# Cross-entropy over 32000 columns: the labels' logits by a masked sum on VectorE, with a third buffer, a fixed order and short loads at both ends

## Chip, cores, metric

One core of a Trainium2 chip. The metric is the time on the device in microseconds (us), the median of several runs. A profiled execution gives a page and a trace; its span is about 1.8 us shorter than the time of the same execution.

## The reference

```python
batch, seq, vocab = 16, 512, 32000            # logits float32, labels integer
logits_max = np.max(logits, axis=-1, keepdims=True)
log_sum_exp = np.log(np.sum(np.exp(logits - logits_max), axis=-1)) + logits_max.squeeze(-1)
loss = -(logits - log_sum_exp[..., None])[np.arange(batch)[:, None], np.arange(seq), labels]
```

There are 8192 rows of 32000 logits: 1.05 GB to read once. For each row the kernel needs the log of the sum of exp, and one single logit, that of the label. Logits are drawn from a normal distribution, so both kernels leave out the maximum.

## The kernel before

A partition holds 64 rows; "group" g is row g of every partition (128 rows). A group is loaded in two pieces of 128x16000, the last three groups in pieces of 128x4000. ScalarE takes exp in place and sums it on the way. The labels' logits come by 64 indirect DMAs (gathers) of 128 single numbers.

```python
data_pool = ctx.enter_context(tc.tile_pool(name="data", bufs=2))     # 128x16000
fine_pool = ctx.enter_context(tc.tile_pool(name="fine", bufs=5))     # 128x4000
nc.sync.dma_start(out=labs64[:], in_=labels_pg)
# ... idx = row * V + label
for g in range(G):
    nc.gpsimd.indirect_dma_start(out=lab_logit[:, g:g + 1], out_offset=None, in_=lg,
        in_offset=bass.IndirectOffsetOnAxis(ap=idx[:, g:g + 1], axis=1))
for g in range(G):
    # the last three groups: the same in 8 pieces of WF = 4000 from fine_pool
    for c in range(C):
        t = data_pool.tile([P, W], FP32)                             # W = 16000
        nc.sync.dma_start(out=t[:], in_=lg_pg[:, g, c * W:(c + 1) * W])
        nc.scalar.activation(out=t[:], in_=t[:], func=Exp, accum_out=stats_col(g, c))
# ... finalize(): sum of stats, Ln on ScalarE, minus lab_logit, store
finalize(0, G - 1)
finalize(G - 1, G)
```

The softmax here doesn't subtract the row's maximum and nothing guards it: scores larger than these inputs give would overflow.

## Time and profile before

| | before |
|---|---|
| median time | 2440.22 us (2440.01 to 2440.32) |
| span of the profiled execution | 2438.7 us |
| bytes from memory | 1048.7 MB, 430 GB/s over the span |
| share of the 16 DMA engines taken by the load queue | 99.6% |

The profile's page of the kernel before: busy time by engine (us, share, instructions), and the DMA queues (packets, MB, share of 16 engines' time). Queue q1 carries the loads, q0 the gathers, q14 the instructions that the engines fetch.

```profile
span 2438.7 us, 851 instructions
...
DVE 1.7 (0%) x5; ACT 1754.4 (72%) x298; POOL 61.2 (3%) x70
...
## 3 DMA queue, kind: packets, MB, share of 16 engines
q1 hardware_dynamic: 21168, 1048.65, 99.6%
q0 software_dynamic: 2048, 0.04, 0.1%
...
q14 instruction: 6, 0.05, 0.0%
```

ScalarE is busy for 72% and VectorE hardly at all (1.7 us): the transfers set the time. This is the table of stretches for before: the stretch, its length, busy time of VectorE, ScalarE and GpSimd (instructions), granted clock, DMA share, GB/s.

```profile
core 0: us, DVE busy (x) ACT busy (x) POOL busy (x), PEclk, DMA share, GB/s
0.00:100.00 100.00, 0.48 (x1) 55.80 (x9) 27.25 (x34) 1.00 1.00 419
100.00:200.00 100.00, 0.00 (x0) 70.85 (x11) 22.62 (x24) 1.00 0.99 421
200.00:300.00 100.00, 0.00 (x0) 72.68 (x11) 11.31 (x12) 1.00 1.01 430
300.00:1300.00 1000.00, 0.00 (x0) 719.74 (x107) 0.00 (x0) 1.00 1.00 433
```

The first 300 us, in which GpSimd issues the gathers, move 419 to 430 GB/s; after that it is 433 throughout. The DMA share is 0.99 to 1.01 in all: the engines hardly wait, but the packets take longer. The packet records of the trace say it more sharply. A row of a 16000-wide load is one packet of 64000 bytes; its mean is 2.424, 2.399 and 2.389 us in the three stretches of 100 us with gathers, and 2.365 us from then on.

The end of the timeline of before: start, duration, engine, line, operation, and in brackets what the engine had waited for. The last exp and the store that ends the kernel:

```profile
2430.84 3.54 ACT L76 ACTIVATE tf<-tf 128x4000 f32<-128x4000 f32 x1 [1.11 <-DMA tf<-in_logits_dram]
...
2436.21 0.34 ACTq L109 DMA_DIRECT2D out_dram<-res  x1
```

The last load lands at 2430.84 us; the span ends 7.9 us later.

### The profile page before, as it was taken

Reading aid. Unit: us, or ns where it says so; the run is one execution under the profiler, and the core shown is the slowest. Engines: PE = TensorE matmul, PEld = TensorE weight load, DVE = VectorE, ACT = ScalarE, POOL = GpSimd, SP = SyncE. Lnnn points to the kernel's source line nnn. Section 1 sums busy time; section 2 is a strip of 40 time slices with the busy share of each in tenths; the row PEclk is TensorE's granted clock in tenths of the full one; section 3 lists DMA queues with packets and bytes.
Section 4 is the critical chain, followed back from the end, with each engine's and each line's share of the span. In section 5 each row is a group of like instructions: output and inputs, shape, how many; then the busy total and the mean of one; then the engine's idle time right before and its main releaser. Section 6 shows DMA issues by size and latency. Waiting matters only on the chain.

```text
span 2438.7 us, 851 instructions
## 1 busy us (share of the span) xinstructions
DVE 1.7 (0%) x5; ACT 1754.4 (72%) x298; POOL 61.2 (3%) x70
## 2 busy tenths in 40 slices
DVE  0000000000000000000000000000000000000000
ACT  4777766777677767777677767777677767777697
POOL 3222000000000000000000000000000000000000
DMA  9999999999999999999999999999999999999998
GB/s 404 437 420 422 435 437 435 429 429 437 437 436 428 431 435 437 435 432 428 435 436 436 435 427 434 436 437 435 427 432 436 437 435 425 434 437 432 426 430 360
DMA packets 23510, 1048.77 MB, mean 430 GB/s; under 512 B 4688, under 2 KB 4816, under 8 KB 4816
## 3 DMA queue, kind: packets, MB, share of 16 engines
q1 hardware_dynamic: 21168, 1048.65, 99.6%
q0 software_dynamic: 2048, 0.04, 0.1%
q10 hardware_dynamic: 288, 0.03, 0.0%
q14 instruction: 6, 0.05, 0.0%
HBM read 1048.67 MB, written 0.03 MB: 430 GB/s over the span
## 4 chain that ended last, share of the span: by engine, by line
DMA 63%; ACT 36%; issue 0%; ACTq 0%; SPq 0%; DVE 0%
DMA t<-in_logits_dram 61%; ACT t L85 34%; DMA tf<-in_logits_dram 2%; ACT tf L76 2%; ACT L101 0%; ACT L76 0%; ACTq L85 0%; ACT logsum L101 0%; SPq L84 0%; DVE res L105 0%; SPq L48 0%; ACTq L109 0%; ACTq L76 0%
## 5 line engine op out<-in xcount | busy, mean ns | idle before, releaser
L85 ACT ACTIVATE t<-t 128x16000 f32<-128x16000 f32 x122 | 1651.4, 13536 | 642.9 <-DMA t<-in_logits_dram 642.9
L76 ACT ACTIVATE tf<-tf 128x4000 f32<-128x4000 f32 x24 | 84.7, 3530 | 14.6 <-DMA tf<-in_logits_dram 14.6
L57 POOL DMA_INDIRECT lab_logit<-in_logits_dram,idx x64 | 60.5, 945 | 186.8 <-DMA lab_logit<-in_logits_dram,idx 184.2
L85 ACT ACTIVATION_READ_ACCUMULATOR t<-t 128x1 f32 x122 | 22.7, 186 | 0.0
L85 ACT ACT_TABLE_LOAD x1 | 1.3, 1283 | 23.3 <-DMA t<-in_logits_dram 23.3
L76 ACT ACTIVATION_READ_ACCUMULATOR tf<-tf 128x1 f32 x24 | 4.5, 187 | 0.0
L101 ACT ACT_TABLE_LOAD x2 | 2.6, 1283 | 0.0
L96 DVE TENSOR_REDUCE totals<-stats 128x63 f32<-128x504 f32 x1 | 0.7, 678 | 2394.9 <-ACT tf L76 2394.9
L76 ACT ACT_TABLE_LOAD x1 | 1.3, 1283 | 0.8 <-DVE res L105 0.8
L66 DVE MEMSET stats<- 128x504 f32 x1 | 0.5, 478 | 0.9 <-PEq L127 0.9
L101 ACT ACTIVATE logsum<-totals 128x63 f32<-128x63 f32 (+1 forms) x2 | 0.5, 229 | 0.0
L105 DVE TENSOR_TENSOR res<-logsum,lab_logit 128x63 f32<-128x63 f32 (+1 forms) x2 | 0.4, 192 | 2.2 <-ACT logsum L101 2.2
L53 POOL TENSOR_TENSOR idx<-idx,labs 128x64 int32<-128x64 int32 x1 | 0.3, 318 | 1.8 <-DMA labs<-in_labels_dram 1.8
L96 DVE TENSOR_REDUCE totals<-stats_last 128x1 f32<-128x8 f32 x1 | 0.2, 161 | 36.4 <-ACT tf L76 36.4
L51 POOL IOTA idx<- 128x64 int32 x1 | 0.2, 172 | 0.4 <-PEq L138 0.4
L127 POOL MEMSET const-uint8-127<- 128x1 uint8 x1 | 0.1, 118 | 0.0
L127 POOL MEMSET const-bfloat16-1.0<- 128x1 bf16 x1 | 0.1, 113 | 0.0
L127 POOL MEMSET const-float32-0.0<- 128x1 f32 x1 | 0.1, 98 | 0.2 <-issue 0.2
L127 POOL MEMSET const-float32-1.0<- 128x1 f32 x1 | 0.1, 104 | 0.0
## 6 DMA issues: line engine op xcount, KB each, us to landing
t<-in_logits_dram SPq DMA_DIRECT2D x122, 8000.0 KB, 24.1
tf<-in_logits_dram SPq DMA_DIRECT2D x24, 2000.0 KB, 20.1
lab_logit<-in_logits_dram,idx POOLq DMA_INDIRECT x64, 33.4
labs<-in_labels_dram SPq DMA_DIRECT2D x1, 64.0 KB, 1.9
out_dram<-res ACTq DMA_DIRECT2D x1, 31.5 KB, 9.1
out_dram<-res ACTq DMA_DIRECT2D x1, 0.5 KB, 1.4
```

What stands on the lines that cost most here:

```text
L51: nc.gpsimd.iota(idx[:], pattern=[[V, G]], base=0, channel_multiplier=G * V)
L53: nc.gpsimd.tensor_tensor(out=idx[:], in0=idx[:], in1=labs32, op=mybir.AluOpType.add)
L57: nc.gpsimd.indirect_dma_start(out=lab_logit[:, g:g + 1], out_offset=None, in_=lg, in_offset=bass.IndirectOffsetOnAxis(ap=idx[:, g:g + 1], ...
L66: nc.vector.memset(stats[:], 0.0)
L76: nc.scalar.activation(out=tf[:], in_=tf[:], func=mybir.ActivationFunctionType.Exp, accum_out=stats_col(g, c),)
L85: nc.scalar.activation(out=t[:], in_=t[:], func=mybir.ActivationFunctionType.Exp, accum_out=stats_col(g, c),)
L96: nc.vector.reduce_sum(out=totals[:, lo:hi], in_=stats[:, lo:hi, :] if hi <= G - 1 else stats_last[:], axis=mybir.AxisListType.X,)
L101: nc.scalar.activation(out=logsum[:, lo:hi], in_=totals[:, lo:hi], func=mybir.ActivationFunctionType.Ln,)
L105: nc.vector.tensor_tensor(out=res[:, lo:hi], in0=logsum[:, lo:hi], in1=lab_logit[:, lo:hi], op=mybir.AluOpType.subtract,)
L127: nc = _bacc.Bacc("TRN2", target_bir_lowering=False, num_devices=1)
```

## The change

The intent: take the label logits out of the data that pass through the chip anyway, on the idle VectorE. For 4000 columns at a time, VectorE compares the column number with the label and multiplies the outcome with the logits; the sum is the label's logit or zero. That saves 62 of the 64 gathers. Around it: a third wide buffer, three short loads first, ten shrinking loads last, exp in halves of 8000 (each waits for two masked sums, as exp overwrites the logits), one table set for exp and log (ScalarE loads a table four times in before, 1.28 us each, and once in after), and program order on all engines. Core of the diff:

```diff
-    data_pool = ctx.enter_context(tc.tile_pool(name="data", bufs=2))
-    fine_pool = ctx.enter_context(tc.tile_pool(name="fine", bufs=5))
+    GG = G - 2
+    plan(0, [[4000, 4000, 8000], [16000]], [(0, 0), (0, 1), (0, 2), (1, 0)])
+    for g in range(1, G - 2):
+        plan(g, [[W], [W]], [(0, 0), (1, 0)])
+    plan(G - 2, [[W], [10000, 6000]], [(0, 0), (1, 0), (1, 1)])
+    plan(G - 1, [[7400, 5840, 2260], [4540, 3720, 2920, 1780, 1460, 1120], [960]], ...)
+    data = ctx.enter_context(tc.tile_pool(name="data", bufs=3))
+    masked = psum.tile([P, H], FP32)                      # H = 4000
+    cols = persist.tile([P, H], mybir.dt.uint16)          # 0 .. 3999
-    nc.sync.dma_start(out=labs64[:], in_=labels_pg)
+    nc.scalar.dma_start(out=labs64[:], in_=labels_pg)
+    nc.scalar.preload_act_table_set("natural_log_exp_and_others")
-    for g in range(G):
+    for g in range(GG, G):
         nc.gpsimd.indirect_dma_start(...)
...
+        nc.sync.dma_start(out=t[:, at:at + n], in_=lg_pg[:, g, c0:c0 + n])
+        if g < GG:
+            for i in range(n // H):
+                h = c0 // H + i
+                lo = at + i * H
+                nc.vector.scalar_tensor_tensor(
+                    out=masked[:], in0=cols[:], scalar=lab_at[:, h, g:g + 1],
+                    in1=t[:, lo:lo + H], op0=ALU.is_equal, op1=ALU.mult,
+                    accum_out=found[:, g, h:h + 1])
+                if n == W and i % 2 == 1:
+                    exp(g, t[:, lo - H:lo + H])
+            if n < W:
+                exp(g, t[:, at:at + n])
+        else:
+            exp(g, t[:, at:at + n])
...
+    nc.scalar.activation(out=logsum_last[:], in_=sums_last[:, K - 1:K], func=LN, bias=part[:])
```

More of the change, by code (lines that the diff above doesn't have):

```diff
@@ L7 @@
 from concourse._compat import with_exitstack
+from concourse.masks import make_identity
 FP32 = mybir.dt.float32
 I32 = mybir.dt.int32
+EXP = mybir.ActivationFunctionType.Exp
+LN = mybir.ActivationFunctionType.Ln
+ALU = mybir.AluOpType
+X = mybir.AxisListType.X
 @with_exitstack
@@ L23 @@
     B, S, V = logits.shape
-    N = B * S
     P = 128
-    G = N // P
-    assert N % P == 0
+    G = B * S // P
     W = 16000
-    C = V // W
-    assert V % W == 0
-    WF = 4000
-    CF = V // WF
-    FINE_GROUPS = 3
-    assert V % WF == 0
+    H = 4000
+    NH = V // H
     lg = logits.rearrange("b s v -> (b s) v")
@@ L41, with plan @@
     out_pg = out.rearrange("b s -> (b s)").rearrange("(p g) -> p g", g=G)
-    data_pool = ctx.enter_context(tc.tile_pool(name="data", bufs=2))
-    fine_pool = ctx.enter_context(tc.tile_pool(name="fine", bufs=5))
+    GG = G - 2
+    loads = []
+    def plan(g, widths_by_buffer, order):
+        n_buffers = 1 + max((l[1] for l in loads), default=-1)
+        for b, i in order:
+            ws = widths_by_buffer[b]
+            loads.append((g, n_buffers + b, sum(ws[:i]), ws[i]))
+    plan(0, [[4000, 4000, 8000], [16000]], [(0, 0), (0, 1), (0, 2), (1, 0)])
@@ L45 @@
+    for g in range(1, G - 2):
+        plan(g, [[W], [W]], [(0, 0), (1, 0)])
+    plan(G - 2, [[W], [10000, 6000]], [(0, 0), (1, 0), (1, 1)])
+    plan(
+        G - 1,
+        [[7400, 5840, 2260], [4540, 3720, 2920, 1780, 1460, 1120], [960]],
+        [(0, 0), (0, 1), (1, 0), (1, 1), (1, 2), (0, 2), (1, 3), (1, 4), (1, 5), (2, 0)],
+    )
+    assert sum(l[3] for l in loads) == G * V
+    data = ctx.enter_context(tc.tile_pool(name="data", bufs=3))
     persist = ctx.enter_context(tc.tile_pool(name="persist", bufs=1))
+    psum = ctx.enter_context(tc.tile_pool(name="psum", bufs=1, space=bass.MemoryType.PSUM))
@@ L47 @@
+    masked = psum.tile([P, H], FP32)
     labs64 = persist.tile([P, G], mybir.dt.int64)
-    nc.sync.dma_start(out=labs64[:], in_=labels_pg)
-    idx = persist.tile([P, G], I32)
-    nc.gpsimd.iota(idx[:], pattern=[[V, G]], base=0, channel_multiplier=G * V)
     labs32 = labs64[:].bitcast(I32).rearrange("p (g two) -> p g two", two=2)[:, :, 0]
-    nc.gpsimd.tensor_tensor(out=idx[:], in0=idx[:], in1=labs32, op=mybir.AluOpType.add)
+    cols = persist.tile([P, H], mybir.dt.uint16)
+    idx = persist.tile([P, G - GG], I32)
@@ L55 @@
+    lab_at = persist.tile([P, NH, G], FP32)
+    found = persist.tile([P, GG, NH], FP32)
     lab_logit = persist.tile([P, G], FP32)
-    for g in range(G):
+    K = 10
+    sums = persist.tile([P, G - 1, 5], FP32)
+    sums_last = persist.tile([P, K], FP32)
+    totals = persist.tile([P, G - 1], FP32)
+    logsum = persist.tile([P, G - 1], FP32)
+    res = persist.tile([P, G - 1], FP32)
+    part = persist.tile([P, 1], FP32)
+    logsum_last = persist.tile([P, 1], FP32)
+    res_last = persist.tile([P, 1], FP32)
@@ L57 @@
+    ctx.enter_context(tc.manual_schedule())
+    nc.scalar.dma_start(out=labs64[:], in_=labels_pg)
+    nc.scalar.preload_act_table_set("natural_log_exp_and_others")
+    nc.vector.memset(sums[:], 0.0)
+    nc.gpsimd.iota(cols[:], pattern=[[1, H]], base=0, channel_multiplier=0)
+    nc.gpsimd.iota(idx[:], pattern=[[V, G - GG]], base=GG * V, channel_multiplier=G * V)
+    nc.gpsimd.tensor_tensor(out=idx[:], in0=idx[:], in1=labs32[:, GG:G], op=ALU.add)
+    for g in range(GG, G):
         nc.gpsimd.indirect_dma_start(
@@ L60 @@
             in_=lg,
-            in_offset=bass.IndirectOffsetOnAxis(ap=idx[:, g:g + 1], axis=1),
+            in_offset=bass.IndirectOffsetOnAxis(ap=idx[:, g - GG:g - GG + 1], axis=1),
         )
-    stats = persist.tile([P, G - 1, CF], FP32)
-    stats_last = persist.tile([P, 1, CF], FP32)
-    nc.vector.memset(stats[:], 0.0)
-    def stats_col(g, c):
-        return stats[:, g, c:c + 1] if g < G - 1 else stats_last[:, 0, c:c + 1]
-    for g in range(G):
-        if g >= G - FINE_GROUPS:
-            for c in range(CF):
-                tf = fine_pool.tile([P, WF], FP32)
-                nc.sync.dma_start(out=tf[:], in_=lg_pg[:, g, c * WF:(c + 1) * WF])
-                nc.scalar.activation(
-                    out=tf[:], in_=tf[:],
-                    func=mybir.ActivationFunctionType.Exp,
-                    accum_out=stats_col(g, c),
-                )
-        else:
-            for c in range(C):
-                t = data_pool.tile([P, W], FP32)
-                nc.sync.dma_start(out=t[:], in_=lg_pg[:, g, c * W:(c + 1) * W])
-                nc.scalar.activation(
-                    out=t[:], in_=t[:],
-                    func=mybir.ActivationFunctionType.Exp,
-                    accum_out=stats_col(g, c),
-                )
@@ L91 @@
-    totals = persist.tile([P, G], FP32)
-    logsum = persist.tile([P, G], FP32)
-    res = persist.tile([P, G], FP32)
-    def finalize(lo, hi):
-        nc.vector.reduce_sum(
-            out=totals[:, lo:hi],
-            in_=stats[:, lo:hi, :] if hi <= G - 1 else stats_last[:],
-            axis=mybir.AxisListType.X,
-        )
-        nc.scalar.activation(
-            out=logsum[:, lo:hi], in_=totals[:, lo:hi],
-            func=mybir.ActivationFunctionType.Ln,
-        )
-        nc.vector.tensor_tensor(
-            out=res[:, lo:hi], in0=logsum[:, lo:hi], in1=lab_logit[:, lo:hi],
-            op=mybir.AluOpType.subtract,
-        )
-        nc.scalar.dma_start(out=out_pg[:, lo:hi], in_=res[:, lo:hi])
@@ L111, with exp @@
-    finalize(0, G - 1)
-    finalize(G - 1, G)
+    for h in range(NH):
+        nc.vector.tensor_scalar(
+            out=lab_at[:, h, :], in0=labs32, scalar1=float(-h * H), scalar2=None, op0=ALU.add
+        )
+    buffers = {}
+    col = {}
+    n_exp = {}
+    def exp(g, ap):
+        k = n_exp.get(g, 0)
+        n_exp[g] = k + 1
+        s = sums[:, g, k:k + 1] if g < G - 1 else sums_last[:, k:k + 1]
+        nc.scalar.activation(out=ap, in_=ap, func=EXP, accum_out=s)
+    for j, (g, b, at, n) in enumerate(loads):
+        if b not in buffers:
+            buffers[b] = data.tile([P, W], FP32, tag="t", name="t")
+        t = buffers[b]
+        c0 = col.get(g, 0)
+        col[g] = c0 + n
+        nc.sync.dma_start(out=t[:, at:at + n], in_=lg_pg[:, g, c0:c0 + n])
[4 more added lines that the diff above has]
+                nc.vector.scalar_tensor_tensor(
+                    out=masked[:],
+                    in0=cols[:],
+                    scalar=lab_at[:, h, g:g + 1],
+                    in1=t[:, lo:lo + H],
+                    op0=ALU.is_equal,
+                    op1=ALU.mult,
+                    accum_out=found[:, g, h:h + 1],
+                )
+                if n == W and i % 2 == 1:
+                    exp(g, t[:, lo - H:lo + H])
+            if n < W:
+                exp(g, t[:, at:at + n])
+        else:
+            exp(g, t[:, at:at + n])
+        left = len(loads) - 1 - j
+        if left == 6:
+            nc.vector.reduce_sum(out=totals[:], in_=sums[:], axis=X)
+            nc.vector.reduce_sum(out=lab_logit[:, 0:GG], in_=found[:], axis=X)
+        if left == 4:
+            nc.scalar.activation(out=logsum[:], in_=totals[:], func=LN)
+            nc.vector.tensor_tensor(out=res[:], in0=logsum[:], in1=lab_logit[:, 0:G - 1], op=ALU.subtract)
+        if left == 1:
+            nc.vector.reduce_sum(out=part[:], in_=sums_last[:, 0:K - 1], axis=X)
@@ L116 @@
+    assert n_exp[G - 1] == K
+    nc.sync.dma_start(out=out_pg[:, 0:G - 1], in_=res[:])
+    nc.scalar.activation(out=logsum_last[:], in_=sums_last[:, K - 1:K], func=LN, bias=part[:])
+    nc.vector.tensor_tensor(out=res_last[:], in0=logsum_last[:], in1=lab_logit[:, G - 1:G], op=ALU.subtract)
+    nc.sync.dma_start(out=out_pg[:, G - 1:G], in_=res_last[:])
 _INS = ['logits', 'labels']
```

## The prediction

> **What bounds the kernel now.** The logit loads do. The page: load queue 99.6% of 16 DMA engines, ScalarE 72%, VectorE nothing. In the trace's packet records every row of a 16000-wide load is one 64000-byte packet. From 300 us on it takes 2.365 us, and the engines hold packets without a gap (idle under 0.1 us per 100 us). That is 16 x 64000 B / 2.365 us = 433 GB/s. [...] The chain of waits shows exp (36%) between loads (63%) only because each load waits for an exp; it is still issued 5 us before its predecessor lands. 128 loads x 8 packets x 2.365 us = 2422 us is the floor. The span is 2438.7 us, so only about 17 us are open.
>
> **Where those 17 us are.**
> 1. Gathers. In the first 300 us, while the 64 indirect gathers run, the packets take 2.424, 2.399 and 2.389 us (per 100 us). The excess over 2.365, summed, over 16 engines, is 4.5 us.
> 2. Start: the label load is issued first on SyncE, the first logits at 1.18 us; the first packet starts at 2.3 us.
> 3. End (timeline): the last 4000-wide load lands at 2430.8 us; exp 3.54, accumulator read 0.19, table load 1.28, log 0.20, subtract 0.16, store 0.34 and about 2.1 us to its end follow: 7.9 us.
> 4. The 24 short loads: 0.597 us per 16000 bytes instead of 0.591, 1.1 us.
>
> **The change.** It removes 62 of 64 gathers: -4.5 us. The label load moves to ScalarE's queue: logits leave 0.4 us sooner. Exp and log share one table set loaded at the start: -1.28 us at the end. The last load is 960 wide: its exp is estimated from 3.54 us at 4000 wide and 13.54 at 16000 (0.2 us + 0.833 ns per column) at 1.0 us, -2.5 us, less about 0.3 us that ScalarE will lag behind the shrinking loads. A third wide buffer and exp in halves only add slack: there is no packet gap to close.
>
> It adds 496 masked sums of 128x4000 on VectorE. In this trace a reduce of 504 columns takes 678 ns and one of 8 takes 161: 153 ns + 1.04 ns per column. At that rate a masked sum is 4.32 us, some 4.4 with the accumulator read; four per load are 17.6 us against 18.9 us of transfer. VectorE becomes over 90% busy but stays off the critical path: the second half's exp ends about 25 us after landing, while the two loads queued behind it take 37.8.
>
> **Predicted time.** 2440.3 - 4.5 - 0.4 - 3.5 - 0.6 (small idle and short loads) = 2431.3 us, range 2427 to 2436. Faster by over 2%: 1%; within 2%: 95%; slower by over 2%: 4%.
>
> **What would show it.** DMA share still over 99%; packets at 2.365 us from the start, no slow first 300 us; VectorE near 90%, masked sums at 4.3 to 4.5 us; ScalarE about 73%; the chain of waits nearly all loads; last landing to end near 4.4 us.
>
> **What would make it wrong.** The masked sum above 4.73 us: then VectorE sets the pace. [...]

That the steady 2.365 us per packet of before are a floor was the author's estimate; that a packet cannot be faster was not shown. In the traces of before and after no 64000-byte packet took less than 2.359 us.

## The result, and the profile after

The time went to 2441.64 us (2441.46 to 2441.81), from 2440.22. The ratio is 1.0006, 95% interval 0.9992 to 1.002: the same. A ratio here is the mean time of one kernel's fast runs over that of the other's of the same rounds, so not quite the ratio of the medians. "Within 2%" was right, but that says little: nothing moves the time by more than 0.4%. The time lies 10.3 us above the one predicted and outside the range.

The page of after, the lines that answer to those of before, and its costliest group (line, engine, operation, shapes, count, busy us, mean ns, idle before it and what ended that):

```profile
span 2440.0 us, 2116 instructions
...
DVE 2211.2 (91%) x1006; ACT 1784.5 (73%) x527; POOL 13.3 (1%) x9
...
q1 hardware_dynamic: 20304, 1048.62, 99.4%
q14 instruction: 16, 0.13, 0.0%
...
L133 DVE SCALAR_TENSOR_TENSOR masked<-cols,lab_at,t 128x4000 f32<-128x4000 uint16 x496 | 2179.4, 4394 | 156.5 <-DMA t<-in_logits_dram 143.5
```

VectorE came out as expected: 91% busy, a masked sum 4.39 us, and with the read of its accumulator about 4.49 us from start to start. Four of them take 17.95 us against 18.9 us between two loads. What is new is q14: 16 packets of instructions in place of 6, the count of a program of 2116 instructions in place of 851. Their share still reads 0.0%.

The chain of waits that ended last, before and then after (share of the span by engine):

```profile
DMA 63%; ACT 36%; issue 0%; ACTq 0%; SPq 0%; DVE 0%
```

```profile
DMA 81%; DVE 16%; ACT 2%; issue 1%; DVEq 0%; SPq 0%
```

The prediction had "nearly all loads" here; VectorE's masked sums stand in the chain with 16%. That alone does not say that they cost time: with the sums cut to 64 columns (e2 below) the loads land only 0.5 us earlier.

The stretches of after, same columns:

```profile
0.00:100.00 100.00, 74.00 (x42) 52.90 (x18) 13.29 (x9) 1.00 1.00 428
100.00:200.00 100.00, 93.53 (x43) 74.01 (x22) 0.00 (x0) 1.00 1.00 432
200.00:300.00 100.00, 94.53 (x43) 72.27 (x21) 0.00 (x0) 1.00 1.00 431
300.00:1300.00 1000.00, 938.27 (x423) 735.40 (x212) 0.00 (x0) 1.00 1.00 434
```

The gain that was expected is there: 432 GB/s where before had 421, and in the packet records 2.366 us per packet from the start. Summed over all logit packets and divided by 16 engines, the transfers take 2424.2 us in place of 2428.1. So 4 us were saved, and more than that was lost again.

The same table for the last stretches, after first, then before:

```profile
2420.00:2424.00 4.00, 0.00 (x0) 4.00 (x3) 0.00 (x0) 1.00 0.73 297
2424.00:2428.00 4.00, 0.00 (x0) 4.00 (x3) 0.00 (x0) 1.00 0.09 39
2428.00:2432.00 4.00, 0.08 (x1) 4.00 (x6) 0.00 (x0) 1.00 0.06 25
```

```profile
2420.00:2424.00 4.00, 0.00 (x0) 2.86 (x3) 0.00 (x0) 1.00 1.03 440
2424.00:2428.00 4.00, 0.00 (x0) 2.87 (x3) 0.00 (x0) 1.00 1.01 432
2428.00:2432.00 4.00, 0.00 (x0) 2.88 (x3) 0.00 (x0) 1.00 0.17 72
```

One sixteenth is 0.0625. From 2424 us on, after's DMA share is 0.09 and 0.06: about one engine of 16 is still at work for eight microseconds (at first a second one too), while the others have nothing left to do. In before all stay busy until 2428 us. The packet records of the last load (128 packets over 16 engines; on the late engine eight of them lie one behind another, 0.15 us each) say when the engines end. The records kept here do not name the engine; packets are taken as one engine's when one starts as the other ends:

```
end of the last logit packet, by engine (us from the span's start)
after   one engine 2431.89   a second 2425.86   a third 2424.18   the others by 2423.2
before  all between 2428.4 and 2430.33
```

So one DMA engine is about 9 us late. It became late in steps: in the trace of after, the first masked sum of a load starts 18.90 us after that of the load before, except about every 14th time, when it is 19.87. Each step comes just after an instruction fetch. Records around the first one (microseconds; the logit packets before and after it follow without a gap, so they are taken as the same engine's):

```
start 119.09  took 2.361  64000 bytes  q1
start 121.45  took 0.324   8192 bytes  q14 (instructions)
start 121.76  took 3.024  64000 bytes  q1     <- 0.66 longer than its neighbours
start 124.78  took 2.369  64000 bytes  q1
```

Nine of the 16 fetches look like this, 265 to 285 us apart: 0.32 us for the fetch and 0.66 us for the packet behind it, 0.98 us together. In 14 loads VectorE runs 56 masked sums, 56 accumulator reads and some 15 waits, 127 instructions. So these nine come at the pace of VectorE's program, one to about 127 instructions; that they are VectorE's is shown below by e4 (seven packets are left without the masked sums) and e1 (ten more with 1098 further instructions on VectorE). The other seven lengthen the packet behind them by only 0.37 to 0.41 us (about 0.7 us together); five of them come at the pace of ScalarE's program (475 to 492 us apart; its two exps, two accumulator reads and a wait per load are some 130 instructions in 26 loads). Nine times 0.98 us are 8.8 us, and the late engine ends 8.7 us after the thirteen (2431.89 against 2423.2): all nine fetches went over one DMA engine. On several engines the nine delays would not have added up, as e4 shows for two (5.5 us in place of 8.8). A load counts as landed only when the last engine has moved its part (the last exp of before starts 0.5 us after the last packet of all, 2430.84 against 2430.33), so each of these fetches delays every later load.

The second loss shows in after's timeline. Call the last masked load 61b (the second piece of group 61). Its first masked sum, the two exps that follow its last one, the last exp and the store:

```profile
2356.27 4.39 DVE L133 SCALAR_TENSOR_TENSOR masked<-cols,lab_at,t 128x4000 f32<-128x4000 uint16 x1 [0.98 <-DMA t<-in_logits_dram]
...
2374.22 6.87 ACT L120 ACTIVATE t<-t 128x8000 f32<-128x8000 f32 x1 [1.96 <-DVE masked L133]
...
2381.08 13.52 ACT L120 ACTIVATE t<-t 128x16000 f32<-128x16000 f32 x1
...
2435.98 0.99 ACT L120 ACTIVATE t<-t 128x960 f32<-128x960 f32 x1
...
2437.61 0.34 SPq L163 DMA_DIRECT2D out_dram<-res_last  x1
```

The exp of 61b's second half can only start at 2374.22 us, when its last masked sum is done, and ends at 2381.08. The first load of group 62 had landed by then, at about 2375.2 us (an estimate: 2356.27 us, when 61b's first masked sum began, and one load's time, 18.9 us). From 2381.08 to 2437 us ScalarE never idles. The last load's packets end at 2431.9 us, but its exp starts only at 2435.98. Landing (about 2432.4, an estimate: the last packet's end and the 0.5 us that before shows from there to the exp) to the end of the span takes 7.6 us. Predicted were 4.4.

### The profile page after: what moved, and what is told of

Its sections match the earlier page's. It is cut to its first block, busy times and chain, and to the rows that moved or that the text cites. A ratio compares the mean times of both kernels' runs of the same rounds, so it can differ in the third digit from the quotient of the medians.

```text
span 2440.0 us, 2116 instructions
## 1 busy us (share of the span) xinstructions
DVE 2211.2 (91%) x1006; ACT 1784.5 (73%) x527; POOL 13.3 (1%) x9
## 4 chain that ended last, share of the span: by engine, by line
DMA 81%; DVE 16%; ACT 2%; issue 1%; DVEq 0%; SPq 0%
DMA t<-in_logits_dram 81%; DVE masked L133 16%; ACT t L120 2%; DVEq L133 0%; SPq L128 0%; ACT logsum_last L161 0%; DVE res_last L162 0%; ACT logsum L154 0%
## 5 line engine op out<-in xcount | busy, mean ns | idle before, releaser
L133 DVE SCALAR_TENSOR_TENSOR masked<-cols,lab_at,t 128x4000 f32<-128x4000 uint16 x496 | 2179.4, 4394 | 156.5 <-DMA t<-in_logits_dram 143.5
L120 ACT ACTIVATE t<-t 128x8000 f32<-128x8000 f32 (+4 forms) x262 | 1759.7, 6716 | 651.7 <-issue 373.4
L133 DVE DVE_READ_ACCUMULATOR masked<-cols,lab_at,t 128x1 f32 x496 | 70.6, 142 | 0.0
L120 ACT ACTIVATION_READ_ACCUMULATOR t<-t 128x1 f32 x262 | 48.8, 186 | 0.0
L100 POOL DMA_INDIRECT lab_logit<-in_logits_dram,idx x2 | 9.3, 4654 | 0.9 <-POOL idx L98 0.5
```

What stands on the lines that cost most here:

```text
L120: nc.scalar.activation(out=ap, in_=ap, func=EXP, accum_out=s)
L133: nc.vector.scalar_tensor_tensor(out=masked[:], in0=cols[:], scalar=lab_at[:, h, g:g + 1], in1=t[:, lo:lo + H], op0=ALU.is_equal, op1=ALU. ...
```

## The experiments

Theory A: the fetches of VectorE's instructions, all on one DMA engine, delay every load, and the kernel ends by as much later. Theory B: behind the last masked group ScalarE has a backlog that it cannot work off before the end. Rival R1: all was lost through the masked sums' own time. Rival R2: VectorE's streaming slows the transfers. The first four ran on one chip (before: 2440.14 us), the last three on one chip (before: 2440.26 us); after itself was timed earlier, beside a before of 2440.22 us. The 95% interval of a ratio is about 0.17% (4 us) to each side. The differences below are read from medians whose runs agree within 0.6 us, and from the traces.

### e1_before_tiny: before, with 1098 useless copies on VectorE

```diff
+    tiny = persist.tile([P, 1], FP32)
+
+                for _ in range(9):
+                    nc.vector.tensor_copy(out=tiny[:], in_=stats_col(g, c))
```

> The kernel before, with 9 copies of one element on VectorE after each wide load (1098 in all). They do no work, nobody waits for them, VectorE was idle. Theory A (each 128 VectorE instructions cost one 8 KB instruction fetch on one DMA engine, which delays that engine, and so every later load, by about 0.98 us): about 9 further fetches, all on one engine; about one wide load in 13 lands 0.9 to 1.0 us late; the time rises by 6 to 9 us, to 2446 to 2449. Rival R1 (the time after was lost by the masked sums' own time, through ScalarE's backlog at the end) and R2 (VectorE's streaming of 128x4000 tiles slows the transfers): no change, 2440.2 within 0.5.

Measured: 2448.58 us, 8.4 us slower, as theory A says. From the page, and the group of the copies:

```profile
DVE 170.2 (7%) x1103; ACT 1754.5 (72%) x298; POOL 61.2 (3%) x70
...
q14 instruction: 16, 0.13, 0.0%
```

```profile
L93 DVE COPY tiny<-stats 128x1 f32<-128x1 f32 x1098 | 168.5, 153 | 2169.2 <-ACT t L87 2135.5
```

The copies keep VectorE busy for 7% of the span, and no load or exp waits for them. The instruction packets go from 6 to 16, so ten are new. In the packet records nine of them are followed by a packet of 3.02 to 3.06 us, and about every 13th wide load lands 0.9 to 1.0 us late; the tenth (2323.8 us) meets the short loads, and the packet behind it takes 1.26 us in place of 0.60. Ten times 0.98 us are 9.8 us, 1.4 us more than measured; f3 shows where most of that went. Neither R1 nor R2 can explain this: there is no masked sum here at all.

### e2_after_narrow: after, with masked sums over 64 columns

```diff
-                    out=masked[:],
-                    in0=cols[:],
+                    out=masked[:, 0:64],
+                    in0=cols[:, 0:64],
-                    in1=t[:, lo:lo + H],
+                    in1=t[:, lo:lo + 64],
```

> The kernel after, with each masked sum over 64 columns in place of 4000 (a wrong result on purpose). Same instructions, same waits, VectorE nearly idle. Theory A: the late landings stay (9 fetches, the last load lands at about 2432); only the backlog of ScalarE at the end goes, about 3.5 us; time 2437.5 to 2438.5. R1 or R2 alone: the whole loss goes, 2431 to 2432.

Measured: 2437.85 us. Its output is wrong, which doesn't matter for the time. VectorE is nearly idle, the fetches are unchanged:

```profile
DVE 177.4 (7%) x1006; ACT 1771.6 (73%) x527; POOL 6.1 (0%) x9
...
q14 instruction: 16, 0.13, 0.0%
```

The last logit packet still ends at 2431.4 us (2431.9 in after), with nine long packets behind fetches. Only 3.8 us came back, nearly all of it at the end: the last exp starts at 2431.92 us, with no backlog. The masked sums' length is therefore not what makes the loads late, and their data do not slow the transfers by more than that half microsecond (R2 falls). It is their number that counts.

### e3_after_gg61: after, with one more group gathered

```diff
-    GG = G - 2
+    GG = G - 3
```

> The kernel after, with 61 groups masked in place of 62; three groups take the gather. A correct result. Theory B (ScalarE enters the last groups about 6 us behind, because its last masked half waits 18 us for VectorE, and 64000 columns of exp after that take as long as the transfers): with one more unmasked group it catches up, the last exp starts within 0.5 us of its landing, last landing to end falls from about 8 to 4.5 us; time 2437.5 to 2438.7. If the end is set by the late DMA engine alone: no change, 2441.6.

Measured: 2437.88 us, a correct result, 3.8 us faster than after. The end of its timeline:

```profile
2422.71 2.64 ACT L120 ACTIVATE t<-t 128x2920 f32<-128x2920 f32 x1 [0.17 <-DMA t<-in_logits_dram]
...
2431.88 1.00 ACT L120 ACTIVATE t<-t 128x960 f32<-128x960 f32 x1
```

The first line shows that the exp of 2920 columns waits again for its load (0.17 us), so ScalarE has caught up, and the last exp starts half a microsecond after the last packet's end (2431.34 us). The loads are as late as in after. This is theory B alone, and it agrees with e2 to 0.03 us.

### e4_after_nomask: after without masked sums

```diff
+    nc.vector.memset(found[:], 0.0)
-            for i in range(n // H):
-                h = c0 // H + i
-                lo = at + i * H
-                nc.vector.scalar_tensor_tensor(
-                    out=masked[:],
-                    in0=cols[:],
-                    scalar=lab_at[:, h, g:g + 1],
-                    in1=t[:, lo:lo + H],
-                    op0=ALU.is_equal,
-                    op1=ALU.mult,
-                    accum_out=found[:, g, h:h + 1],
-                )
-                if n == W and i % 2 == 1:
-                    exp(g, t[:, lo - H:lo + H])
+            if n == W:
+                exp(g, t[:, 0:W // 2])
+                exp(g, t[:, W // 2:W])
```

> The kernel after without any masked sum (a wrong result on purpose; exp in halves stays). Theories A and B together: no VectorE fetches, no backlog; the last load lands at about 2425.5 (5 ScalarE fetches of about 0.7 us on another engine still delay it by some 3 us), the end 4.5 us later; time 2431 to 2433. If something else in the change cost the time (third buffer, short loads, exp in halves): it stays above 2436.

Measured: 2432.58 us, 9.1 us below after. Its output is wrong, which doesn't matter for the time.

```profile
span 2430.5 us, 996 instructions
...
q14 instruction: 7, 0.06, 0.0%
```

The page shows seven instruction packets, none of VectorE's kind. The last packet ends at 2425.92 us on one engine, 2424.07 on a second, and between 2422.2 and 2423.2 on the others (mean 2422.6). The first lag, 3.3 us behind that mean, is about that of five fetches of 0.69 us (3.4 us), which are put down to ScalarE by their pace in after; the next fits two. Lags on different engines do not add: from e2 to e4 the last packet comes 5.5 us earlier, not 8.8, because the engine with these five fetches is now the late one.

### f1_postexp: the masked sum after exp, in place, over 8000 columns

The lines that differ, without those around them (in the new order exp stands once, ahead of the masked sums):

```diff
-    H = 4000
+    H = 8000
-    plan(0, [[4000, 4000, 8000], [16000]], [(0, 0), (0, 1), (0, 2), (1, 0)])
+    plan(0, [[8000, 8000], [16000]], [(0, 0), (0, 1), (1, 0)])
-    psum = ctx.enter_context(tc.tile_pool(name="psum", bufs=1, space=bass.MemoryType.PSUM))
-    masked = psum.tile([P, H], FP32)
-    sums = persist.tile([P, G - 1, 5], FP32)
+    sums = persist.tile([P, G - 1, 3], FP32)
+        exp(g, t[:, at:at + n])
-                    out=masked[:],
+                    out=t[:, lo:lo + H],
-                if n == W and i % 2 == 1:
-                    exp(g, t[:, lo - H:lo + H])
-            if n < W:
-                exp(g, t[:, at:at + n])
-        else:
-            exp(g, t[:, at:at + n])
+        if left == 9:
+            nc.vector.reduce_sum(out=lab_logit[:, 0:GG], in_=found[:], axis=X)
+        if left == 7:
+            nc.scalar.activation(out=lab_logit[:, 0:GG], in_=lab_logit[:, 0:GG], func=LN)
-            nc.vector.reduce_sum(out=lab_logit[:, 0:GG], in_=found[:], axis=X)
```

> The kernel after with the order turned round: exp first, in one piece for each load and in place, then the masked sum over 8000 columns of exp, in place too (no separate output tile), and the log of what it found at the end. A correct result. Half as many masked sums, with one wait each: about 510 VectorE instructions, so 4 fetches of 0.98 us in place of 9; ScalarE no longer waits for VectorE, so no backlog at the end. Theories A and B: last load lands at about 2426.5 to 2427.5, end 4.6 us later; time 2432 to 2434. If the late engine were not due to VectorE's instruction count: last landing stays near 2432, time 2437 to 2438.

Measured: 2433.12 us, a correct result, ratio to before 0.9971 (0.9958 to 0.9985), and better than both kernels, by 0.3%.

```profile
DVE 2114.2 (87%) x506; ACT 1748.8 (72%) x280; POOL 9.4 (0%) x9
...
q14 instruction: 9, 0.07, 0.0%
...
L132 DVE SCALAR_TENSOR_TENSOR t<-cols,lab_at,t 128x8000 f32<-128x8000 uint16 x248 | 2111.1, 8550 | 255.7 <-ACT t L118 249.3
```

VectorE still does the same work (87% busy) and needs half the instructions (506 in place of 1006). Four fetches of its kind are left, and the last logit packet ends at 2426.48 us. Since exp no longer waits for VectorE, there is no backlog at the end:

```profile
2409.92 3.99 ACT L118 ACTIVATE t<-t 128x4540 f32<-128x4540 f32 x1 [0.32 <-DMA t<-in_logits_dram]
...
2427.02 0.99 ACT L118 ACTIVATE t<-t 128x960 f32<-128x960 f32 x1
```

### f2_gather64: all labels gathered, with the rest of the change

The same file without cols, masked, lab_at, found and the masked sums. In short:

```diff
-    GG = G - 2
+    GG = 0
-        if g < GG:
-            ... masked sums and exp in halves ...
-        else:
-            exp(g, t[:, at:at + n])
+        exp(g, t[:, at:at + n])
```

> The kernel after with all 64 labels gathered as before and no masked sum; exp in one piece. It has the change's start, third buffer, end and table set, not its VectorE work. A correct result. By the sum: no VectorE fetches, 3 or 4 ScalarE fetches (2 to 2.8 us on one engine), the gathers' 4.5 us on all engines back: time 2434.5 to 2436.5. Below 2433 the gathers cost less than I read from before; above 2438 there is a cost in the rest of the change that e4 did not show.

Measured: 2435.68 us, correct. The six fetches cost about 0.7 us each; the last packet ends at 2429.08 us. So the new start, end and third buffer are worth 4.6 us with all the gathers kept, and the masked sums as f1 has them another 2.6 us in place of the gathers.

### f3_before_tiny_pool: the useless copies on GpSimd

```diff
-                    nc.vector.tensor_copy(out=tiny[:], in_=stats_col(g, c))
+                    nc.gpsimd.tensor_copy(out=tiny[:], in_=stats_col(g, c))
```

> The kernel before with the 1098 one-element copies of e1 on GpSimd in place of VectorE. If it is the instruction fetch of any engine that delays loads: 9 or 10 further fetches, time 2446 to 2450. If it is something of VectorE alone: 2440 to 2441.

Measured: 2444.69 us, 4.4 us slower than before. My number was missed: I had reckoned with VectorE's 0.98 us. Nine further fetches are there, but the packet behind each takes 2.71 us, so that one costs about 0.66 us, 5.9 us for nine. The 1.5 us between these 5.9 us and the 4.4 measured are mostly in the traces. In before, two of ScalarE's own fetches (1204 and 2018 us, put down to it by their pace: 813 us, or 43 loads of three ScalarE instructions each) make a load 0.67 us late each. In f3 and in e1 those fetches are still there, but no load is late at those places: another engine, the one with the added fetches, is the last by then. That is 1.3 us, of the 1.5 here and of the 1.4 in e1. That a fetch of another engine than VectorE delays loads is shown; that it costs as much is not true.

## Why the prediction was wrong

- **"It removes 62 of 64 gathers: -4.5 us."** Right: 3.9 us less packet time per engine, after the few short loads, and 2.366 us per packet from the start.
- **The start, 0.4 us sooner.** Right: the first logit packet starts at 1.75 us in place of 2.27.
- **VectorE's speed.** Right: 4.39 us was within the 4.3 to 4.5 predicted, over 90% busy. The 1.04 ns per column that the prediction took from the reduces of before held for the sums of a uint16 and an fp32 source: 4.394 us for 4000 columns into PSUM (after) and 8.55 us for 8000 in place in SBUF (f1), 1.04 ns per further column.
- **"VectorE becomes over 90% busy but stays off the critical path."** This is the step that failed. It holds for VectorE's data and not for its instructions. The sum had no term for instruction fetches. The term is 9 x 0.98 us = 8.8 us on one DMA engine; from e2 to e4, where it is taken away and ScalarE's own 3.4 us remain, it is worth 5.3 us of time. The table of queues could not warn of it: it averages over 16 engines, and the fetches are 0.0% there. The packet records of before could have: they hold six fetches with long packets behind them, and I did not look at those.
- **"Less about 0.3 us that ScalarE will lag behind the shrinking loads."** The second term that was mis-sized: it was about 3.6 us (2435.98 against 2432.4), measured as 3.8 by e2 and by e3. I had checked that the late exp leaves the buffers free in time (25 us against 37.8), and not that the unmasked groups' exps queue behind it. From 2381 us ScalarE had 64000 columns to do, 56 us of work, and the last load landed only about 51 us later.
- Together: 5.3 + 3.8 = 9.1 us, the way from after to e4 (2432.58 us). This sum is no check of its own, as e2 stands between the two; the check is that e3 gives the 3.8 us a second time. That after came out level with before is chance: the rest of the change gains 7.6 us (before to e4), and these two lose 9.1. The rest, 1.3 us to the 2431.3 predicted, I put down to the 3.4 us of ScalarE's fetches, of which some had been in before; that part is argued, not shown.
- R1 explains the 3.8 us alone, and R2 nothing: e2 keeps the instructions, drops 98% of the data, and the loads land within 0.5 us of where they did.

What stays open: why VectorE's fetch lengthens the packet behind it by 0.66 us and the others by 0.34 (f3) to 0.41 us.

## What to carry to other kernels

When transfers fill the time, as here, an instruction on an idle engine is not free (1098 useless copies took 8.4 us in e1 and 4.4 us in f3): in these runs every 128 or so were one 8 KB fetch on one DMA engine, which cost that engine 0.66 us (GpSimd) to 0.98 us (VectorE), and a load was as late as its latest engine. So count instructions and prefer few wide ones (f1 did the same work with half of them). An average over 16 engines hides this; look at when loads land, and at how many engines are busy at the very end. And when work is put in front of a serial engine, follow its backlog to the last instruction, not only to the release of the buffers.
